# A two-layer diffusion backbone on one core: who forms h in the opening phase, and on which queue the later modulation weights are loaded

## The chip, the cores and the metric

The kernel runs on one core of one Trainium2 chip. The metric is the device time of one execution in microseconds (us): the median of several executions of the whole program. "About what can be told from no change" in the prediction means 1% of that time, some 15 us.

The core has five sequencers that run their own instruction lists in order and wait for each other through semaphores: TensorE (PE; its weight loads have a row of their own, PEld), VectorE (DVE), ScalarE (ACT), GpSimd (POOL) and SyncE (SP). DMAs are issued by SP, ACT or POOL, each on its own queue (SPq, ACTq, POOLq); a DMA that has to wait holds back everything behind it on the list of the engine that issues it.

## The reference, cut to what matters

Two layers work on 512 latent tokens (x) and 256 context tokens (ctx) of width 1024. The first thing that is computed is the adaptive norm of layer 0, then the first projections and the low-rank inputs of the RWKV branch:

```python
shift, scale, gate = jnp.split(s_lat @ mod_w[i] + mod_b[i], 3, axis=-1)
h = rms_norm(x, g_pre[i]) * (1.0 + scale[:, None]) + shift[:, None]
shift_c, scale_c, gate_c = jnp.split(s_ctx @ mod_w[i] + mod_b[i], 3, axis=-1)
hc = rms_norm(ctx, g_pre[i]) * (1.0 + scale_c) + shift_c
...
rc, kc, vc, zac, bc, cc, xc, zbc = jnp.split(hc @ w_in, EVEN_SPLITS, axis=-1)
r, k, v, za, bg, cg, xb, zb = jnp.split(h @ w_in, EVEN_SPLITS, axis=-1)
...
dh = centred_shift(h) - h            # 0.5 * (left + right) - h
xw = h + dh * mu_wa[0]
xa = h + dh * mu_wa[1]
lw = einsum(tanh(einsum(xw, w1)), w2)
la = einsum(einsum(xa, a1), a2)
```

After that come the bidirectional scan, a gated short convolution, the output projection, and layer 1 (a Conformer convolution module); neither is touched by the change.

## The kernel before, in words

**Precision.** Large products are made from split operands: `x = xh + xl`, where `xh` is `x` rounded to the matmul format fp32r and `xl` the rest. `mm3` (L59) runs three matmuls for one product: high by high (L60), high by low (L61), low by high (L62). So for each operand ScalarE casts the high part and another engine subtracts to get the low part; for weights that is `hilo` (L120: DMA, cast at L125, subtraction at L126 on the engine that `env["lo"]` names).

**The opening, `start()` (L208).** The columns of parameters are loaded on ACT's queue and transposed on PE. Six token tiles (two of ctx, four of x) are loaded on SP's queue (L226, L228). Then 16 loads of 512 KB bring the shift and scale parts of `mod_w` of layer 0 (L235, SP's queue) through six buffers (`mws`: four slices of the tile ectx, and mw4, mw5), each consumed by matmuls into the PSUM bank `mp` (L237). Meanwhile the tokens are normed (L242 to L245) and transposed into eight channel tiles `hp[kt]` (L253, L254), 770 columns each with zero columns for the shift at both ends of each stream. When `mp` is complete it is copied to SBUF (L256 on VectorE, L257 on ScalarE), transposed (L260, into `mt`), and gives the columns `modc0` (L261) and `gsc0` (L265). With them h is formed, first for ctx (8 tiles of 256 columns), then for the latents (8 of 512): the scaling of `hp[kt]` in place (L272 on ScalarE for odd latent tiles, L274 on VectorE for all others), the cast to the high part (L277, ScalarE; tile hctx or hlh), and the subtraction for the low part (L278, VectorE; tile hctx or hll).

**What follows.** `load_w(8, "k0")` (L839) loads the first projection weight (tile wrk, two halves of 256 KB) and splits it; for this one weight GpSimd does the subtraction (`lo_for`, L332). `start_w1` (L290) loads the low-rank weights (eight DMAs of 128 KB, L296) and four constants (L298 to L301). `prep_ctx(0, rest)` (L380) runs four projections (k0, k1, v0, v1): each a ctx product (`pck`, `pcv`: 24 matmuls of 256 columns) and a latent product (`plk`, `plv`: 24 of 512 columns), with the neighbour mix `shifted` behind each (L353 to L356). Between them `rest` (L847) works through the remaining 16 groups of modulation weights, which h does not need: four DMAs of 256 KB on POOL's queue (L856; tiles mwo, in the buffer that mw5 used, and mwr) and eight small matmuls into `uh` or `mpb` (L858). Then `lora` (L304): for each of eight channel tiles GpSimd adds the left and right neighbours (L310), VectorE forms `dh` (L311) and twice `xw = dh * mu + h` into one of four slots of the tile E1 (its name in the profile is ectx, L314), and PE multiplies each `xw` with its low-rank weight (`pwl`/`pal` and `pwc`, L317 and L318).

**What sets the order.** The code is traced in program order, and a scheduler of the framework then orders each engine's list by priority (program order) and by when it believes operands and buffers to be there. So a later piece can stand ahead of an earlier one on an engine's list: the matmuls of `rest` stand among those of `mp`, for example. `tc.issue_after(ins)` adds an edge, so that whatever the block traces on the engine of `ins` stands behind `ins` on that engine's list. `env["last"]` is, in the changed kernel, the last of the 16 `mod_w` DMAs of L235.

Of the kernel before, what the change touches and what calls it, by code (L numbers as in the profile page):

```python
# [10 lines left out]
AF = mybir.ActivationFunctionType  # L11
ALU = mybir.AluOpType
# [3 lines left out]
P = 128  # L16
D = 1024
# [34 lines left out]
def kernel(ctx: ExitStack, tc: tile.TileContext, I: dict, out: bass.AP):  # L52
# [129 lines left out]
    def small(name, shape):  # L182
        return cvp.tile(shape, F32, tag=name, name=name)

    ones = small("ones", [P, 1])
    G.memset(ones, 1.0)
    omu, hmu, hka, oka = (small(n, [P, k]) for n, k in (("omu", 24), ("hmu", 24), ("hka", 8), ("oka", 8)))
    blk = small("blk", [P, P])
    ctr = small("ctr", [P, P])
    maskE = small("maskE", [P, 3, P])  # L190
# [17 lines left out]
    def start():  # L208
        for gi, (grp, tag) in enumerate(zip(COLS, ("P", "kk", "kd", "a"))):
            rw = w(tag, f"rows{gi}")  # L210
            n_all = 0
            for nm, n in grp:
                src = colsrc[nm]
                while len(src.shape) > 1:
                    src = src.rearrange("a b -> (a b)" if len(src.shape) == 2 else "a b c -> (a b c)")
                nc.scalar.dma_start(rw[n_all : n_all + n, 0:P], src.rearrange("(a b) -> a b", b=P))
                n_all += n
            pt = ps_at(f"rowsT{gi}")
            T.transpose(pt[:, :n_all], rw[:n_all, 0:P], ident[:n_all, :n_all])
            V.tensor_copy(colt[gi], pt[:, :n_all])  # L220
            if gi == 0:
                S.activation(s2[:, :, 0], col("c", 0, 8), AF.Silu)
                S.activation(s2[:, :, 1], col("c_ctx", 0, 8), AF.Silu)
        tokt = [w("AR", f"tok{j}") for j in range(6)]
        for j in range(2):
            nc.sync.dma_start(tokt[j], I["ctx"][0, j * P : (j + 1) * P, :])  # L226
        for j in range(4):
            nc.sync.dma_start(tokt[2 + j], I["x"][0, j * P : (j + 1) * P, :])  # L228
        mws = [E1[:, D * q : D * q + D] for q in range(4)] + [w("X", "mw4"), w("O", "mw5")]
        mp = ps.tile([P, 512], F32, tag="zo", name="mp", bufs=2)  # L230
        V.memset(mp, 0.0)
        for kt in range(KT):
            for b in range(2):
                mw = mws[(2 * kt + b) % 6]
                nc.sync.dma_start(mw, I["mod_w"][0, kt * P : (kt + 1) * P, b * D : b * D + D])  # L235
                for q in (2 * b, 2 * b + 1):
                    mm(mp[32 * q : 32 * q + 2, :], s2[:, kt, :], mw[:, q % 2 * 512 : q % 2 * 512 + 512],  # L237
                       kt == 0, kt == KT - 1)
        hp = [w(t, f"hp{k}")[:, 0:D] for k, t in enumerate(("UV", "UV", "BKt", "BKt", "BKt", "BKt", "BK", "BK"))]
        for j in range(6):  # L240
            rs = ss6[:, 8 + j : 9 + j]
            S.activation(hp[7], tokt[j], AF.Square, accum_out=ss6[:, j : j + 1])  # L242
            S.activation(rs, ss6[:, j : j + 1], AF.Sqrt, bias=epsr[:, 0:1], scale=1.0 / D)
            V.reciprocal(rs, rs)
            V.tensor_scalar(out=tokt[j], in0=tokt[j], scalar1=rs, scalar2=None, op0=ALU.mult)  # L245
        for kt in range(KT):
            for c0, cn in ((0, 1), (257, 2), (771, 1)):
                G.memset(hp[kt][:, c0 : c0 + cn], 0.0)
        for kt in range(KT):
            for (j0, nj, o0) in ((0, 2, 1), (2, 4, 259)):  # L250
                pt = ps_mm(f"xt{kt}_{j0}")
                for j in range(nj):
                    T.transpose(pt[:, j * P : (j + 1) * P], tokt[j0 + j][:, kt * P : (kt + 1) * P], ident)  # L253
                S.copy(hp[kt][:, o0 : o0 + nj * P], pt[:, : nj * P])  # L254
        mrow = E1[:, 0:512]
        V.tensor_copy(mrow[:, 0:256], mp[:, 0:256])  # L256
        S.copy(mrow[:, 256:512], mp[:, 256:512])  # L257
        mt = ps_at("mt")
        for j in range(4):
            T.transpose(mt[:, j * P : (j + 1) * P], mrow[:, j * P : (j + 1) * P], ident)  # L260
        V.tensor_tensor(out=modc0.rearrange("p (q j) b -> p q j b", q=4),  # L261
                        in0=mt.rearrange("p (j q x) -> p q j x", j=4, q=4)[:, :, :, 0:2],
                        in1=col("mod_b0", 0, 16).rearrange("p (q j) -> p q j", q=4).unsqueeze(3).to_broadcast([P, 4, 4, 2]),
                        op=ALU.add)
        V.scalar_tensor_tensor(out=gsc0, in0=modc0[:, 8:16, :], scalar=1.0,  # L265
                               in1=col("g_pre0", 0, 8).unsqueeze(2).to_broadcast([P, 8, 2]),
                               op0=ALU.add, op1=ALU.mult)
        for (z, n, d0) in ((1, CTX, 1), (0, SEQ, 259)):
            for kt in range(KT):
                hv = hp[kt][:, d0 : d0 + n]  # L270
                if z == 0 and kt % 2:
                    S.activation(hv, hv, AF.Identity, scale=gsc0[:, kt, z : z + 1], bias=modc0[:, kt, z : z + 1])  # L272
                else:
                    V.tensor_scalar(out=hv, in0=hv, scalar1=gsc0[:, kt, z : z + 1],  # L274
                                    scalar2=modc0[:, kt, z : z + 1], op0=ALU.mult, op1=ALU.add)
                dh_, dl_ = (hch, hcl) if z else hlat
                S.copy(dh_[:, kt, :], hv)  # L277
                V.tensor_tensor(out=dl_[:, kt, :], in0=hv, in1=dh_[:, kt, :], op=ALU.subtract)  # L278
        V.tensor_scalar(out=omu, in0=col("mu_rkv", 0, 24), scalar1=-1.0, scalar2=1.0, op0=ALU.mult, op1=ALU.add)
        V.tensor_scalar(out=hmu, in0=col("mu_rkv", 0, 24), scalar1=0.5, scalar2=None, op0=ALU.mult)  # L280
        V.tensor_scalar(out=hka, in0=col("k_a", 0, 8), scalar1=0.5, scalar2=None, op0=ALU.mult)
        V.tensor_scalar(out=oka, in0=hka, scalar1=-1.0, scalar2=1.0, op0=ALU.mult, op1=ALU.add)
        ho = 0
        for nmh, nh in (("w0", 16), ("a0", 16), ("lnx_w", 8), ("lnx_b", 8), ("sc_w", 24)):
            V.tensor_scalar(out=hcol[:, ho : ho + nh], in0=col(nmh, 0, nh), scalar1=0.5, scalar2=None, op0=ALU.mult)
            half[nmh] = ho
            ho += nh
        return hp
# [15 lines left out]
    def lora(hp, w1, between):  # L304
        pwl, pal = (ps.tile([P, 512], F32, tag="zo", name=n, bufs=2) for n in ("pwl", "pal"))
        pwc = ps_at("pwc")
        for kt in range(KT):
            h1 = hp[kt][:, 1:771]
            dh = w("AR", f"dh{kt}")[:, 0:770]
            G.tensor_tensor(out=dh, in0=hp[kt][:, 0:770], in1=hp[kt][:, 2:772], op=ALU.add)  # L310
            V.scalar_tensor_tensor(out=dh, in0=dh, scalar=0.5, in1=h1, op0=ALU.mult, op1=ALU.subtract)  # L311
            for (zi, pl) in ((0, pwl), (1, pal)):
                xw = E1[:, (2 * kt + zi) % 4 * D : (2 * kt + zi) % 4 * D + 770]
                V.scalar_tensor_tensor(out=xw, in0=dh, scalar=col("mu_wa", zi * 8 + kt), in1=h1,  # L314
                                       op0=ALU.mult, op1=ALU.add)
                lhs = w1[zi][kt // 4][:, kt % 4].rearrange("p a b -> p (a b)")
                mm(pl, lhs, xw[:, 258:770], kt == 0, kt == KT - 1)  # L317
                mm(pwc[:, zi * CTX : (zi + 1) * CTX], lhs, xw[:, 0:CTX], kt == 0 and zi == 0, kt == KT - 1 and zi == 1)  # L318
            if kt % 2:
                between()  # L320
# [9 lines left out]
                V.tensor_tensor(out=lorl[i][z][lr], in0=t[rows], in1=th[rows], op=ALU.subtract)  # L330

    def lo_for(nm):  # L332
        env["lo"] = G if nm == "k0" else V

    def w_half(src, name):
        raw = wp.tile([P, 512], F32, tag="wr", name="wr" + name, bufs=2)
# [499 lines left out]
        nc.gpsimd.dma_start(ysp[8 + p], yb)  # L836

    hp = start()
    first_w = [load_w(8, "k0")]  # L839
    first = hp, start_w1()  # L840
    lorc_ = w("bon", "lorc")
    lorc = [lorc_[:, 0:CTX], lorc_[:, CTX : 2 * CTX]]
    mwo = w("O", "mwo")
# [3 lines left out]
    def rest(n=1):  # L847
        for g in range(mv["n"], min(mv["n"] + n, 16)):
            half_, kt = g // 8, g % 8
            if kt == 0:  # L850
                mv["acc"] = uhs[0] if half_ == 0 else ps.tile([P, 512], F32, tag="zo", name="mpb", bufs=2)
                V.memset(mv["acc"], 0.0)
            for q in range(4):
                u = 4 * half_ + q
                layer, c0 = (0, 2 * D + 512 * u) if u < 2 else (1, 512 * (u - 2))
                nc.gpsimd.dma_start(mws[q], I["mod_w"][layer, kt * P : (kt + 1) * P, c0 : c0 + 512])  # L856
            for q in range(4):
                mm(mv["acc"][32 * q : 32 * q + 2, :], s2[:, kt, :], mws[q], kt == 0, kt == KT - 1)  # L858
            if kt == KT - 1:
                rested(half_, mv["acc"])  # L860
        mv["n"] += n
# [410 lines left out]
```

## Time and profile before

| | us |
|---|---|
| median of 3 runs | 1514.84 |
| lowest, highest | 1505.89, 1517.57 |
| the profiled execution's own time | 1506.4 |
| its span (first to last instruction) | 1504.6 |
| mean granted TensorE clock in it | 0.978 of full |

The profile is of one execution. A row of the timeline reads: start (us from the span's start), duration, engine, source line, operation, out<-in by tile names, shapes, count; in square brackets, the idle time of the engine before it and what ended that. Neighbouring equal instructions are merged into one row with their count, and the duration then is from the first start to the last end. A row with a q behind the engine's name is the sequencer's, for instance a DMA being issued. A row of the table by stretches gives for each engine the busy time and in brackets the number of instructions, then the granted TensorE clock, the mean busy share of the 16 DMA engines, and GB/s. Durations of matmuls are modelled at their ends: pitches between starts are safer.

### The profile page before, as it was taken

Reading aid. Unit: us, or ns where it says so; the run is one execution under the profiler, and the core shown is the slowest. Engines: PE = TensorE matmul, PEld = TensorE weight load, DVE = VectorE, ACT = ScalarE, POOL = GpSimd, SP = SyncE. Lnnn points to the kernel's source line nnn. Section 1 sums busy time; section 2 is a strip of 40 time slices with the busy share of each in tenths; the row PEclk is TensorE's granted clock in tenths of the full one; section 3 lists DMA queues with packets and bytes.
Section 4 is the critical chain, followed back from the end, with each engine's and each line's share of the span. In section 5 each row is a group of like instructions: output and inputs, shape, how many; then the busy total and the mean of one; then the engine's idle time right before and its main releaser. Section 6 shows DMA issues by size and latency. Waiting matters only on the chain.

```text
span 1504.6 us, 29614 instructions
## 1 busy us (share of the span) xinstructions
PE 1429.3 (95%) x11857; PEld 1014.2 (67%) x11857; DVE 964.3 (64%) x2242; ACT 766.4 (51%) x1552; POOL 152.3 (10%) x263
## 2 busy tenths in 40 slices
PE   5699999999998999999999999999999999999998
PEld 1374577878776766666666666677757666688876
DVE  2575587558696978888788887658544525434333
ACT  4323465364755575755757657546553414363322
POOL 0533210000110101011011000001100000000000
PEclk9899999979997999999999999999999999999999
DMA  8644533212232312231222212468403303033222
GB/s 316 174 130 164 162 113 99 89 57 67 80 89 77 89 60 74 67 91 51 80 72 68 79 46 82 152 221 293 159 20 112 103 10 113 28 112 99 94 88 84
DMA packets 136650, 156.59 MB, mean 104 GB/s; under 512 B 15266, under 2 KB 104034, under 8 KB 136512
## 3 DMA queue, kind: packets, MB, share of 16 engines
q1 hardware_dynamic: 119952, 104.37, 22.4%
q0 software_dynamic: 15488, 49.14, 10.1%
q8 instruction: 93, 1.52, 0.4%
q10 hardware_dynamic: 1072, 1.19, 0.2%
q14 instruction: 45, 0.37, 0.1%
HBM read 137.36 MB, written 17.31 MB: 103 GB/s over the span
## 4 chain that ended last, share of the span: by engine, by line
PE 46%; ACT 6%; DVE 5%; DMA 2%; issue 2%; DVEq 0%; SPq 0%; ACTq 0%
PE pu L61 4%; PE pu L62 4%; PE pu L60 4%; PE zol L57 3%; PE uh L57 2%; PE f L61 2%; PE f L60 2%; PE f L62 2%; PE pz L61 2%; PE pz L62 2%; PE pz L60 2%; PE px L57 2%; PE pc L57 1%; PE pal L57 1%; PE o L62 1%
## 5 line engine op out<-in xcount | busy, mean ns | idle before, releaser
L57 PE MATMUL pal<-ARl,BKl 64*128 64x128 f32 x512 | 59.1, 311 | 6.3 <-DVE xtmpc L643 4.3
L645 DVE TENSOR_TENSOR Yl<-Yl,xtmpl 128x126 f32<-128x126 f32 (+22 forms) x248 | 62.5, 252 | 2.2
L643 DVE TENSOR_TENSOR xtmpl<-Xl,Yl 128x126 f32<-128x126 f32 (+22 forms) x248 | 62.4, 252 | 2.0
L57 PEld LDWEIGHTS pal<-ARl,BKl 64*128 64x128 f32 x512 | 44.2, 199 | 25.8 <-DVE E L588 6.2
L57 PE MATMUL zol<-UV,E 64*64 64x64 f32 (+1 forms) x1024 | 54.2, 221 | 0.0
L61 PE MATMUL o<-wl,y 128*128 128x512 f32 x124 | 50.0, 403 | 4.3 <-DVE wl L126 4.3
L57 PE MATMUL zol<-Hl,ARl 64*64 64x64 f32 x896 | 50.2, 230 | 2.3 <-DVE Hl L756 2.3
L1091 DVE TENSOR_TENSOR a<-pu,a 128x512 f32<-128x512 f32 x16 | 11.1, 692 | 62.0 <-PE pu L62 59.7
L749 ACT COPY UV<-uh 64x128 f32<-64x128 f32 x128 | 33.4, 261 | 33.2 <-PE uh L57 30.9
L126 DVE TENSOR_TENSOR wl<-wr,wh 128x1024 fp32r<-128x1024 f32 x28 | 37.1, 1323 | 20.7 <-ACT wh L125 20.5
L588 DVE TENSOR_TENSOR E<-pal,maskE 128x512 f32<-128x512 f32 x64 | 43.5, 685 | 10.4 <-PE pal L57 10.2
L60 PE MATMUL o<-wh,y 128*128 128x512 f32 x124 | 49.6, 401 | 0.5 <-ACT wh L125 0.5
L62 PE MATMUL o<-wh,y 128*128 128x512 f32 x124 | 49.9, 403 | 0.0
L57 PEld LDWEIGHTS zol<-Hl,ARl 64*64 64x64 f32 x896 | 35.0, 133 | 21.2 <-issue 16.9
L1096 ACT CAST ah<-a 64x512 fp32r<-64x512 f32 x32 | 19.8, 620 | 56.3 <-DVE a L1091 55.9
L756 DVE SCALAR_TENSOR_TENSOR Hl<-uh,PCl,HPl 128x64 f32<-128x64 f32 x112 | 26.8, 282 | 30.4 <-PE uh L57 21.4
L57 PEld LDWEIGHTS uh<-UV,BKt 128*64 128x64 f32 x704 | 26.8, 138 | 27.5 <-ACT UV L749 21.5
L57 PEld LDWEIGHTS zol<-UV,E 64*64 64x64 f32 (+1 forms) x1024 | 42.5, 136 | 2.8 <-ACT UV L749 2.1
L125 ACT CAST whcg<-wrcg 128x512 fp32r<-128x512 f32 x16 | 9.9, 621 | 63.5 <-DMA wrcg<-in_ev_w_in_dram 51.2
L57 PE MATMUL uh<-UV,BKt 128*64 128x64 f32 x704 | 36.9, 234 | 3.6 <-ACT UV L749 2.8
L125 ACT CAST wh<-wr 128x1024 fp32r<-128x1024 f32 x28 | 29.4, 1051 | 21.4 <-PE o L61 11.9
L57 PEld LDWEIGHTS uh<-Ol,E 64*64 64x64 f32 x512 | 19.9, 133 | 25.8 <-ACT Ol L743 17.4
(972 smaller groups left out, 4434.6 us busy)
## 6 DMA issues: line engine op xcount, KB each, us to landing
wr<-in_ev_w_out_dram SPq DMA_DIRECT2D x28, 512.0 KB, 5.0
mwr<-in_mod_w_dram POOLq DMA_DIRECT2D x32, 256.0 KB, 4.2
mwo<-in_mod_w_dram POOLq DMA_DIRECT2D x32, 256.0 KB, 3.2
ectx<-in_mod_w_dram SPq DMA_DIRECT2D x12, 512.0 KB, 5.1
wrk<-in_ev_w_in_dram SPq DMA_DIRECT2D x16, 256.0 KB, 2.9
wrv<-in_ev_w_in_dram SPq DMA_DIRECT2D x16, 256.0 KB, 2.9
wrr<-in_ev_w_in_dram SPq DMA_DIRECT2D x16, 256.0 KB, 2.9
wrza<-in_ev_w_in_dram SPq DMA_DIRECT2D x16, 256.0 KB, 2.8
```

The costliest lines, as they stand in the source:

```text
L57: return T.matmul(o, lhsT, rhs, start=start, stop=stop)
L60: T.matmul(o, ah, bh, start=start, stop=False)
L61: T.matmul(o, ah, bl, start=False, stop=False)
L62: T.matmul(o, al, bh, start=False, stop=stop)
L125: S.copy(hi, raw)
L126: env["lo"].tensor_tensor(out=lo, in0=raw, in1=hi, op=ALU.subtract)
L588: V.tensor_tensor(out=E[:, h, z * NLAT + c0 : z * NLAT + c0 + m, :], in0=pas[h], in1=maskE[:, z * (1 + h) : z * (1 + h) + 1, 0:x].to_broad ...
L643: V.tensor_tensor(out=tv, in0=X[:, :i, i : i + 1].to_broadcast([P, i, m]), in1=Y[:, i : i + 1, c0:].to_broadcast([P, i, m]), op=ALU.mult)
L645: V.tensor_tensor(out=Y[:, :i, c0:], in0=Y[:, :i, c0:], in1=tv, op=ALU.add)
L749: u_ = S.copy(UV[ZR[1 - h], i : 2 * nch - i : 2 * nch - 1 - 2 * i, ZR[h]], uh[ZR[1 - h], 0:2, :])
L756: h_ = V.scalar_tensor_tensor(out=Hn[:, z, :], in0=uh[:, 2 + z, :], scalar=PC[z][:, i : i + 1], in1=HP[:, z, :], op0=ALU.mult, op1=ALU.add)
L1096: S.copy(ahl[s][hr], a[hr])
```

## The change

Three things, all before the first stage of the scan. (1) In `start`, ScalarE writes the high part of h directly from `hp` (scale, bias and rounding in one ACTIVATE, 16 in all); VectorE then scales `hp` in place (all 16) and subtracts. The separate casts and the four ScalarE scalings in place are gone. (2) GpSimd's 8 additions (`dh`) go to VectorE, as does the subtraction for k0's weight; `dh` is now the sum of the two neighbours, `xw` is first `(1 - mu) * h` by ScalarE (16 new ACTIVATEs with the columns `owa`) and then `+ 0.5 * mu * dh` by VectorE. The 8 VectorE operations of L311 are gone, so that the number of VectorE operations in `lora` stays at 24. (3) The loads of k0's weight and of `start_w1` are tied behind the last `mod_w` DMA on SP's list, and the first two groups of `rest` (eight DMAs of 256 KB) are issued by SP, also behind it, instead of by POOL.

```diff
@@ start
+    owa, hwa = (small(n, [P, 16]) for n in ("owa", "hwa"))
...
-                nc.sync.dma_start(mw, I["mod_w"][0, kt * P : (kt + 1) * P, b * D : b * D + D])
+                env["last"] = nc.sync.dma_start(mw, I["mod_w"][0, kt * P : (kt + 1) * P, b * D : b * D + D])
...
                 hv = hp[kt][:, d0 : d0 + n]
-                if z == 0 and kt % 2:
-                    S.activation(hv, hv, AF.Identity, scale=gsc0[:, kt, z : z + 1], bias=modc0[:, kt, z : z + 1])
-                else:
-                    V.tensor_scalar(out=hv, in0=hv, scalar1=gsc0[:, kt, z : z + 1],
-                                    scalar2=modc0[:, kt, z : z + 1], op0=ALU.mult, op1=ALU.add)
                 dh_, dl_ = (hch, hcl) if z else hlat
-                S.copy(dh_[:, kt, :], hv)
+                S.activation(dh_[:, kt, :], hv, AF.Identity, scale=gsc0[:, kt, z : z + 1], bias=modc0[:, kt, z : z + 1])
+                V.tensor_scalar(out=hv, in0=hv, scalar1=gsc0[:, kt, z : z + 1],
+                                scalar2=modc0[:, kt, z : z + 1], op0=ALU.mult, op1=ALU.add)
                 V.tensor_tensor(out=dl_[:, kt, :], in0=hv, in1=dh_[:, kt, :], op=ALU.subtract)
...
+        V.tensor_scalar(out=owa, in0=col("mu_wa", 0, 16), scalar1=-1.0, scalar2=1.0, op0=ALU.mult, op1=ALU.add)
+        V.tensor_scalar(out=hwa, in0=col("mu_wa", 0, 16), scalar1=0.5, scalar2=None, op0=ALU.mult)
@@ lora
-            G.tensor_tensor(out=dh, in0=hp[kt][:, 0:770], in1=hp[kt][:, 2:772], op=ALU.add)
-            V.scalar_tensor_tensor(out=dh, in0=dh, scalar=0.5, in1=h1, op0=ALU.mult, op1=ALU.subtract)
+            V.tensor_tensor(out=dh, in0=hp[kt][:, 0:770], in1=hp[kt][:, 2:772], op=ALU.add)
             for (zi, pl) in ((0, pwl), (1, pal)):
                 xw = E1[:, (2 * kt + zi) % 4 * D : (2 * kt + zi) % 4 * D + 770]
-                V.scalar_tensor_tensor(out=xw, in0=dh, scalar=col("mu_wa", zi * 8 + kt), in1=h1,
+                S.activation(xw, h1, AF.Copy, scale=owa[:, zi * 8 + kt : zi * 8 + kt + 1])
+                V.scalar_tensor_tensor(out=xw, in0=dh, scalar=hwa[:, zi * 8 + kt : zi * 8 + kt + 1], in1=xw,
                                        op0=ALU.mult, op1=ALU.add)
@@ lo_for
-        env["lo"] = G if nm == "k0" else V
+        env["lo"] = V
@@ after start
-    first_w = [load_w(8, "k0")]
-    first = hp, start_w1()
+    with tc.issue_after(env["last"].ins):
+        first_w = [load_w(8, "k0")]
+        first = hp, start_w1()
@@ rest
+                if g < 2:
+                    with tc.issue_after(env["last"].ins):
+                        nc.sync.dma_start(mws[q], I["mod_w"][layer, kt * P : (kt + 1) * P, c0 : c0 + 512])
+                    continue
                 nc.gpsimd.dma_start(mws[q], I["mod_w"][layer, kt * P : (kt + 1) * P, c0 : c0 + 512])
```

## The prediction

> **What bounds the kernel now.** I read the page first, then the table by stretches of the opening, and then the timeline by engine around the places where PE idles.
>
> ```profile
> span 1504.6 us, 29614 instructions
> PE 1429.3 (95%) x11857; PEld 1014.2 (67%) x11857; DVE 964.3 (64%) x2242; ACT 766.4 (51%) x1552; POOL 152.3 (10%) x263
> PE   5699999999998999999999999999999999999998
> ```
>
> PE is busy nearly everywhere except in the first two of the 40 slices, that is in the first 75 us. The stretches say what kind of time that is (us; busy us of PE, PEld, DVE, ACT, POOL, each with a count; clock; DMA share; GB/s):
>
> ```profile
> 20.00:40.00 20.00, 19.59 (x92) 5.92 (x88) 4.34 (x9) 9.38 (x24) 0.79 (x5) 1.00 0.91 328
> 55.90:63.00 7.10, 1.92 (x5) 0.46 (x4) 7.06 (x20) 6.95 (x15) 3.02 (x6) 0.94 0.84 249
> 63.00:69.00 6.00, 5.94 (x25) 5.74 (x26) 6.00 (x4) 1.67 (x4) 6.00 (x4) 0.50 0.01 1
> 69.00:76.00 7.00, 4.18 (x17) 2.83 (x16) 7.00 (x8) 2.65 (x5) 3.65 (x3) 0.99 0.00 0
> 84.70:135.00 50.30, 50.30 (x223) 31.86 (x224) 30.04 (x40) 9.75 (x17) 18.08 (x24) 1.00 0.47 151
> ```
>
> From 84.7 to 135 PE has no idle time and its clock is full: it works off the projections and lora, and what comes earlier into that stretch comes out of it earlier. Before it PE waits for h, and h waits for the modulation columns. The chain, on PE and the issuing queues:
>
> ```profile
> 1.85 1.25 POOL L856 DMA_DIRECT2D mwr<-in_mod_w_dram  x2 [0.27 <-issue]
> 31.06 5.29 SPq L235 DMA_DIRECT2D ectx<-in_mod_w_dram  x4
> 36.40 0.98 SPq L122 DMA_DIRECT2D wrk<-in_ev_w_in_dram  x2
> 39.38 1.07 POOL L856 DMA_DIRECT2D mwo<-in_mod_w_dram  x2 [13.00 <-PE mp L57]
> 39.59 1.03 PE L57 MATMUL mp<-ectx,s 128*2 128x512 f32 x4
> 45.79 1.01 PE L57 MATMUL uh<-mwo,s 128*2 128x512 f32 x1 [4.60 <-DMA mwo<-in_mod_w_dram]
> 48.84 1.04 PE L57 MATMUL mp<-ectx,s 128*2 128x512 f32 x5
> 51.46 1.02 PE L57 MATMUL uh<-mwo,s 128*2 128x512 f32 x2 [1.57 <-DMA mwo<-in_mod_w_dram]
> 52.41 0.66 PE L260 MATMUL mt<-ident,ectx 128*128 128x128 f32 x4
> 63.06 0.80 PE L60 MATMUL plk<-hlh,whk 128*128 128x512 f32 x1 [3.86 <-ACT hlh L277]
> 77.65 0.63 PE L61 MATMUL plk<-hll,whk 128*128 128x512 f32 x1
> 78.08 0.63 PE L62 MATMUL plk<-hlh,wlk 128*128 128x512 f32 x1
> ```
>
> Twice a matmul of `rest` (uh), which nobody needs yet, stands on PE's list ahead of what h needs and waits for its own DMA: at 45.79 ahead of the last matmuls of `mp`, at 51.46 ahead of the transposes mt. The mod_w loads themselves were all issued by 36.4.
>
> VectorE carries h from there, up to the last subtraction at 75.47:
>
> ```profile
> 49.94 0.42 DVE L256 COPY ectx<-mp 128x256 f32<-128x256 f32 x1 [22.32 <-DMA maskE<-in_maskE_dram]
> 50.40 0.37 ACT L257 COPY ectx<-mp 128x256 f32<-128x256 f32 x1 [8.57 <-DVE ectx L256]
> 53.10 0.19 DVE L261 TENSOR_TENSOR modc<-mt,cols 128x32 f32<-128x32 f32 x1 [2.74 <-PE mt L260]
> 53.33 2.63 DVE L265 SCALAR_TENSOR_TENSOR gsc<-modc,cols 128x16 f32<-128x16 f32 x1
> 53.41 2.50 POOL L126 TENSOR_TENSOR wlk<-wrk,whk 128x512 fp32r<-128x512 f32 x2
> 55.99 1.49 DVE L274 TENSOR_SCALAR hp<-hp,gsc,modc 128x256 f32<-128x256 f32 x4
> 61.38 0.53 DVE L274 TENSOR_SCALAR hp<-hp,gsc,modc 128x512 f32<-128x512 f32 x1
> 61.84 0.68 DVE L278 TENSOR_TENSOR hll<-hp,hlh 128x512 fp32r<-128x512 f32 x1
> 62.44 1.72 DVE L274 TENSOR_SCALAR hp<-hp,gsc,modc 128x512 f32<-128x512 f32 x1
> 62.42 6.83 POOL L310 TENSOR_TENSOR dh<-hp 128x770 f32<-128x770 f32 x4 [2.18 <-DVE hp L274]
> 64.09 5.71 DVE L278 TENSOR_TENSOR hll<-hp,hlh 128x512 fp32r<-128x512 f32 x3
> 75.47 0.68 DVE L278 TENSOR_TENSOR hll<-hp,hlh 128x512 fp32r<-128x512 f32 x1
> ```
>
> The reader is to see that VectorE stretches whenever GpSimd computes: 16 columns of gsc take 2.63 us beside wlk on POOL, where modc with 32 columns took 0.19; a 512-wide scaling takes 1.72 beside dh against 0.53 alone; three subtractions take 5.71 against 0.68 each. This agrees with the Trainium skill, GPSIMD Engine Reference, Key points, which has the two share SBUF interfaces when VectorE reads two SBUF inputs or runs a 2-port mode.
>
> **The change part by part.** The sum is made against the profiled execution's own 1506.4 us (span 1504.6 and 1.8 around it).
>
> *Step A, the end of mp.* The last four mod_w issues begin at 31.06, the last at 36.0, and a mod_w load lands 5.1 us behind its issue:
>
> ```profile
> L235 SPq DMA_DIRECT2D ectx<-in_mod_w_dram x12: 327/328/432, 12.7 to 36.0; - x12
> DMA to landing us min/median/max: 5.1/5.1/5.1
> ```
>
> So the last is there at 41.1; I take 41.5, since wrk and the low-rank weights follow at once on the same queue and still do. A group of four mp matmuls takes 1.03, with 0.5 for hand-offs mp ends at 43.0 in place of 48.84 + 1.04 = 49.9: **6.9 us gained**, if PE's new order has uh behind mp. I take that, because uh's loads now stand behind wrk, the low-rank weights and the constants on SP, hence later than mp's in any order by readiness. Bounds: 0 (something else not ready stands there), and 8.5 (the 0.5 MB that POOL loads at 1.85 are out of the way: 1.6 us at 328 GB/s, left out since the early matmuls of mp wait for more than data).
>
> The part of the change that ties wrk and the low-rank weights behind mod_w does nothing by itself: on SPq they already are (36.40 behind 31.06 + 5.29). What moves is the eight loads of `rest`: they cost SP eight issues more, some 3.5 us by 1.07 for two on POOL, behind everything h needs. The second four wait on SP for PE to have read the first four (same buffers); behind them wait the issues of k1's and v0's weights. That costs nothing while PE runs uh in its gaps before k0's product ends (the stretch 55.9 to 63 has 5 us of idle PE), and some 6 us once (issue, landing, cast, subtraction) if PE puts uh behind k0.
>
> The Trainium skill, DMA: Bandwidth & Descriptors, Queues, rings and completion order, has each DMA engine alternate between the queues that have work; by it POOL's two early loads take their share from SP's, and step A would be larger; that is the rival "more than forecast".
>
> *Step B, from mp to gsc:* 49.88 to 55.96, 6.1 us. Left are the two copies (0.9 with hand-off, 49.94 to 50.77), 0.3 to PE, the transposes (52.41 to 53.10, 0.7), modc 0.2, gsc 0.2: 2.3. **Gained 3.8**: 1.57 from uh at 51.46, the rest from gsc without POOL beside it.
>
> *Step C, from gsc to the end of k0's products:* 55.96 to 78.71, 22.75 us. VectorE has the same 16 pairs of scaling and subtraction as ever and four more scalings. At paces without POOL: ctx 55.99 to 61.38, 5.4 for eight pairs; a latent pair 61.38 to 62.44, 1.06, eight make 8.5; k0's two weight subtractions, taken over from POOL, 0.6 each by their pitch, 1.2 (61.84 to 62.44). ScalarE's form with fp32r output does not occur in the trace; the rows nearest are the same ACTIVATE with float output and the cast:
>
> ```profile
> L272 ACT ACTIVATE hp<-hp,modc,gsc 128x512 f32<-128x512 f32 x4 | 3.1, 811 | 4.2 <-DVE gsc L265 4.2
> L277 ACT CAST hlh<-hp 128x512 fp32r<-128x512 f32 x8 | 4.7, 616 | 6.7 <-DVE hp L274 6.7
> ```
>
> It lies between 0.62 (a cast alone) and 1.43 (both in a row); I take 0.81, as the arithmetic is that of L272. Then ScalarE, at no more than 16 x 0.81 = 13.0, stays under VectorE's 5.4 + 8.5 = 13.9, and only its first, some 0.6 for half the columns, is on the path; at 1.43 for a latent tile and about 0.8 for a ctx tile it would need 18 and cost 4 us. In-place scaling now waits for ScalarE to have read, which runs ahead. PE's tail behind the last subtraction: 1.0. Sum 5.4 + 8.5 + 1.2 + 0.6 + 1.0 = 16.7: **gained 6.0**.
>
> PE's clock was 0.50 from 63 to 69, behind the 3.86 us wait, and full again from 69. In my sum PE's gaps until k0's end are shorter than that wait, so it is costed at full clock; at half clock it is a rival, below. The Trainium skill, TensorE: Matmul & The Clock Gate, Part 1, states the rule behind these rows, and it speaks against a PE that is fed in drops: half rate after an idle window of some 3.4 us, until a window of as long is busy.
>
> *Step D, lora and behind.* VectorE's 8 operations of L311 become 8 additions of the same width, cost as before; they no longer wait for POOL.
>
> ```profile
> L311 DVE SCALAR_TENSOR_TENSOR dh<-dh,hp x8: 944/948/961, 76.5 to 92.6; 128x770 f32<-128x770 f32 x8
> 115.13 1.02 PE L57 MATMUL pal<-ectx,a 128*128 128x512 f32 x2
> 116.42 1.02 PE L57 MATMUL pwl<-ectx,w 128*128 128x512 f32 x2
> 115.33 1.02 DVE L314 SCALAR_TENSOR_TENSOR ectx<-dh,cols,hp 128x770 f32<-128x770 f32 x1 [0.24 <-PE pwc L57]
> ```
>
> ScalarE gets 16 ACTIVATEs of 770 columns, 0.9 to 1.1 each by the 0.81 for 512; it is busy 9.75 of 50.3 there, so they fit (about 16). Each xw slot goes round in ScalarE 1.0, VectorE 1.0, PE 1.29 and three hand-offs of 0.25, about 4.0 us; with four slots that is 1.0 per unit against PE's 1.29 (115.13 to 116.42), so PE still sets the pace: nothing. One uh group (0.97) that ran in an idle PE now runs in a busy one, and a stall of about that size at 84 goes. Net 0, bounds -2 and +2.
>
> Sum: 6.9 + 3.8 + 6.0 = 16.7, rounded down to 16.5 for the new ops in between: 1506.4 - 16.5 = 1489.9 for an execution like the profiled one. The median shown is 1514.84, 8.4 above it; the median forecast is 1514.8 - 16.5 = **1498.3 us**.
>
> **The rivals.**
>
> *The wait moves on PE's list.* The order is made by estimates of readiness. Evidence for: at 63.06 k0's first latent matmul stood ahead of its ctx ones and held PE 3.86 us, besides the two waits for uh. If one such wait stays, 3.9 to 8 us are kept: gain 8.5 to 12.6, about 1504.
>
> *VectorE becomes the bound.* It takes all of POOL's arithmetic. If the scheduler pulls the eight additions ahead of the latent subtractions, h is later by 8 x 0.95 = 7.6: gain 9, 1506. Against: h is earlier in program order.
>
> *PE stays at half clock.* Fed tile by tile, PE may not count as busy. At half clock a 512-column matmul starts every 0.43 (77.65 to 78.08), so a latent tile's three take 1.29 against VectorE's 1.06: 8 x 0.23 = 1.8 us more and a longer tail, 0.6. Gain 14.1, 1500.7. Against: in the stretch 55.90:63.00 PE was busy 1.92 of 7.10 us at clock 0.94.
>
> *Mod_w does not land earlier, so step A is not there.* If the descriptors behind the last load, not PE's order, hold it until about 45.5, A shrinks to 2 to 3: gain 12, 1503.
>
> *More than forecast.* The 0.5 MB that POOL loads at 1.85 no longer stand ahead of mod_w; at the 328 GB/s of the stretch from 20 that is 1.6 us, and 2 us in D come on top: gain 20, 1495.
>
> *Slower: the slots of lora.* ScalarE writes a slot first and VectorE then completes it; if fewer than the four slots are in flight, because an xw on ScalarE's in-order list is held behind a cast that waits for a weight, the round of 4.0 us shows. With two in flight it is 2.0 per unit, 16 x 0.7 = 11 us, which still leaves a gain; with one, 16 x 2.7 = 43 us and a net loss of 27, 1541. It decides below about 1.8 slots. Against: in the trace four are in flight (the xw at 115.33 follows the pwc four units earlier), and ScalarE is idle four fifths of the time.
>
> **How the numbers follow.** The forecast 0.36; PE at half clock 0.08; PE's order 0.22; VectorE 0.11; mod_w's landing 0.06; more than forecast 0.11; lora slower 0.06. A measurement of this kernel can tell about 1%, 15 us, from no change, and the forecast lies just across that line: of its 0.36 some 0.30 are over 1%, with all of "more", 0.03 of half clock and 0.04 of the others; slower by over 1% is lora's 0.06. So faster 0.48, same 0.46, slower 0.06. The likeliest case alone spans 1493 to 1504. The range takes in the other gains (1509) and the single execution's level at the low end (1490 and a little less): 1487 to 1510.
>
> **What would show it.** The last mp matmul at 43 in place of 49.9, with no DMA wait of uh ahead of it; gsc at 0.2 us, at about 45.5; latent pairs on VectorE at 1.06 throughout; no POOL arithmetic before 100 us; the last k0 matmul near 62; PE without a gap from there to the end of lora, near 118. I would be wrong if PE shows a new wait of over 3 us before k0's end, if VectorE does additions of 770 columns between the latent subtractions, or if PE waits for ScalarE's xw in lora.

## The result and the profile after

The changed kernel takes 1492.43 us (median of 4 runs, 1483.60 to 1499.09) against 1510.37 for the kernel before (4 runs, 1504.58 to 1517.57): a ratio of 0.9887, with a 95% interval of 0.984 to 0.9934. The interval leaves out 1 but holds 0.99, so there is a gain, and whether it is over 1% stays open. The forecast was 1498.3 us with 16.5 gained; 17.9 separate the medians. The profiled execution of the changed kernel is its slowest run, 1499.09 us, so the two traces lie only 7 us apart; a section below says where the other 9 went.

The page of the changed kernel:

```profile
span 1497.3 us, 29614 instructions
PE 1433.0 (96%) x11857; PEld 1014.5 (68%) x11857; DVE 957.5 (64%) x2250; ACT 779.7 (52%) x1564; POOL 125.9 (8%) x245
PE   5999999999989999999999999999999999999998
```

The second slice of PE, which was 6, is 9. The table by stretches of the changed kernel (columns as before: us; busy us of PE, PEld, DVE, ACT, POOL with counts; clock; DMA share; GB/s):

```profile
41.90:44.20 2.30, 0.84 (x4) 0.40 (x4) 1.35 (x5) 1.42 (x4) 0.00 (x0) 1.00 0.87 197
44.20:52.00 7.80, 6.83 (x27) 6.13 (x28) 7.70 (x21) 7.80 (x14) 0.00 (x0) 0.56 0.94 279
52.00:61.30 9.30, 8.88 (x35) 4.13 (x33) 8.76 (x17) 6.60 (x10) 0.35 (x1) 1.00 0.41 130
61.30:76.00 14.70, 14.70 (x89) 10.52 (x88) 12.25 (x17) 4.05 (x7) 2.87 (x6) 1.00 0.77 224
76.00:120.00 44.00, 44.00 (x192) 26.14 (x189) 25.47 (x32) 19.82 (x28) 13.61 (x26) 1.00 0.48 159
```

From the end of mp to that of k0's products POOL does next to nothing, VectorE is busy 17.8 of 19.4 us, ScalarE 15.8 and PE 16.6. Behind it PE has no gap up to 120, past the end of lora. In the timeline of the changed kernel the chain of the prediction reads:

```profile
29.14 5.29 SPq L236 DMA_DIRECT2D ectx<-in_mod_w_dram  x4
34.48 0.99 SPq L122 DMA_DIRECT2D wrk<-in_ev_w_in_dram  x2
40.84 1.03 PE L57 MATMUL mp<-ectx,s 128*2 128x512 f32 x4 [0.60 <-DMA ectx<-in_mod_w_dram]
42.40 0.84 PE L261 MATMUL mt<-ident,ectx 128*128 128x128 f32 x4 [0.53 <-DVE ectx L257]
43.98 0.17 DVE L266 SCALAR_TENSOR_TENSOR gsc<-modc,cols 128x16 f32<-128x16 f32 x1
48.14 5.74 ACT L273 ACTIVATE hlh<-hp,modc,gsc 128x512 fp32r<-128x512 f32 x8
51.28 0.99 DVE L274 TENSOR_SCALAR hp<-hp,gsc,modc 128x512 f32<-128x512 f32 x2
52.20 1.28 DVE L276 TENSOR_TENSOR hll<-hp,hlh 128x512 fp32r<-128x512 f32 x2
58.48 0.68 DVE L276 TENSOR_TENSOR hll<-hp,hlh 128x512 fp32r<-128x512 f32 x1
60.90 0.40 PE L62 MATMUL plk<-hlh,wlk 128*128 128x512 f32 x1
```

No `uh` matmul is left ahead of mp or mt; the last four matmuls of mp wait 0.60 us for their own data. gsc takes 0.17 in place of 2.63, and two latent pairs take 2.12 from 51.28 to 53.40, where the next scaling starts, 1.06 each, as forecast. k0's products end at 61.3 in place of 78.7.

### The profile page after: what moved, and what is told of

It reads as the page before. It is cut to its first block, busy times and chain, and to the rows that moved or that the text cites. A ratio compares the mean times of both kernels' runs of the same rounds, so it can differ in the third digit from the quotient of the medians.

```text
span 1497.3 us, 29614 instructions
## 1 busy us (share of the span) xinstructions
PE 1433.0 (96%) x11857; PEld 1014.5 (68%) x11857; DVE 957.5 (64%) x2250; ACT 779.7 (52%) x1564; POOL 125.9 (8%) x245
## 4 chain that ended last, share of the span: by engine, by line
PE 44%; ACT 7%; DVE 5%; DMA 4%; issue 2%; SPq 0%; DVEq 0%; ACTq 0%
PE pu L61 4%; PE pu L62 4%; PE pu L60 4%; PE zol L57 3%; PE uh L57 2%; PE f L61 2%; PE f L62 2%; PE f L60 2%; PE pz L62 2%; PE pz L61 2%; PE pz L60 2%; PE px L57 2%; PE pal L57 1%; PE pc L57 1%; DMA wrcg<-in_ev_w_in_dram 1%
## 5 line engine op out<-in xcount | busy, mean ns | idle before, releaser
L57 PEld LDWEIGHTS pal<-ARl,BKl 64*128 64x128 f32 x512 | 44.2, 199 | 25.9 <-DVE E L588 6.1
L1096 DVE TENSOR_TENSOR a<-pu,a 128x512 f32<-128x512 f32 x16 | 11.1, 691 | 61.6 <-PE pu L62 59.3
L62 PE MATMUL o<-wh,y 128*128 128x512 f32 x124 | 49.9, 403 | 0.0
L57 PEld LDWEIGHTS zol<-Hl,ARl 64*64 64x64 f32 x896 | 35.1, 133 | 21.3 <-issue 17.1
L756 DVE SCALAR_TENSOR_TENSOR Hl<-uh,PCl,HPl 128x64 f32<-128x64 f32 x112 | 26.6, 280 | 30.7 <-PE uh L57 21.6
```

The source lines that it names most:

```text
L57: return T.matmul(o, lhsT, rhs, start=start, stop=stop)
L62: T.matmul(o, al, bh, start=False, stop=stop)
L756: h_ = V.scalar_tensor_tensor(out=Hn[:, z, :], in0=uh[:, 2 + z, :], scalar=PC[z][:, i : i + 1], in1=HP[:, z, :], op0=ALU.mult, op1=ALU.add)
```

## Experiments

Ten kernels were run. Six of them take the three parts of the change singly and in pairs. Times of one kernel spread by 10 to 20 us, so a ratio (the time against that of the kernel before, with its 95% interval) is good to about 0.004 (6 us) here; the landmarks of the trace separate what the medians can't. Each landmark comes from one execution; the last two rows, which are the same work in the same order, differ by 0.3 us at most. "lora's end" is the end of the last matmul of lora, the gain is against 132.7 in the profile of before, and "PE idle" is PE's idle time in the gaps that begin between 18 us and lora's end.

| kernel | parts | mp ends | gsc ends | k0's products end | lora's end (gain) | PE idle | ratio, interval |
|---|---|---|---|---|---|---|---|
| before | none | 49.9 | 56.0 | 78.7 | 132.7 | 15.9 | |
| e2_act_only | 1 | 49.9 | 55.3 | 80.4 | 135.1 (-2.4) | 17.0 | 1.0035, 0.999 to 1.008 |
| e3_nopool_only | 2 | 49.4 | 52.5 | 73.7 | 122.9 (9.8) | 7.9 | 0.9905, 0.9876 to 0.9934 |
| e1_queue_only | 3 | 42.1 | 44.9 | 68.1 | 127.7 (5.0) | 11.2 | 0.9985, 0.9945 to 1.0024 |
| e4_no_queue | 1, 2 | 49.3 | 52.8 | 79.5 | 129.2 (3.5) | 9.5 | 0.9983, 0.9955 to 1.001 |
| e5_no_poolpart | 1, 3 | 41.2 | 43.9 | 67.4 | 123.5 (9.2) | 8.2 | 0.9941, 0.991 to 0.9972 |
| e6_no_act | 2, 3 | 40.9 | 43.2 | 58.6 | 118.4 (14.3) | 5.1 | 0.991, 0.9877 to 0.9944 |
| after | 1, 2, 3 | 41.9 | 44.2 | 61.3 | 116.9 (15.8) | 3.9 | 0.9887, 0.984 to 0.9934 |
| e8_no_tie | 1, 2, 3 | 42.2 | 44.5 | 61.6 | 117.1 (15.6) | 4.4 | 0.9914, 0.988 to 0.9948 |

**Part 3 alone (e1_queue_only).** From the changed kernel, parts 1 and 2 are undone:

```diff
-                S.activation(dh_[:, kt, :], hv, AF.Identity, scale=gsc0[:, kt, z : z + 1], bias=modc0[:, kt, z : z + 1])
+                S.copy(dh_[:, kt, :], hv)
...
+                if z == 0 and kt % 2:
+                    S.activation(hv, hv, AF.Identity, scale=gsc0[:, kt, z : z + 1], bias=modc0[:, kt, z : z + 1])
+                else:
                     V.tensor_scalar(out=hv, in0=hv, scalar1=gsc0[:, kt, z : z + 1],
                                     scalar2=modc0[:, kt, z : z + 1], op0=ALU.mult, op1=ALU.add)
...
-            V.tensor_tensor(out=dh, in0=hp[kt][:, 0:770], in1=hp[kt][:, 2:772], op=ALU.add)
+            G.tensor_tensor(out=dh, in0=hp[kt][:, 0:770], in1=hp[kt][:, 2:772], op=ALU.add)
+            V.scalar_tensor_tensor(out=dh, in0=dh, scalar=0.5, in1=h1, op0=ALU.mult, op1=ALU.subtract)
-                S.activation(xw, h1, AF.Copy, scale=owa[:, zi * 8 + kt : zi * 8 + kt + 1])
-                V.scalar_tensor_tensor(out=xw, in0=dh, scalar=hwa[:, zi * 8 + kt : zi * 8 + kt + 1], in1=xw,
+                V.scalar_tensor_tensor(out=xw, in0=dh, scalar=col("mu_wa", zi * 8 + kt), in1=h1,
-        env["lo"] = V
+        env["lo"] = G if nm == "k0" else V
```

> The kernel before with part 3 alone: the first two groups of rest on SP, tied behind the last mod_w load; h and lora as before, GpSimd computing. Marks: mp's last matmul ended at 49.9 before and 41.9 after, lora's last matmul at 132.2 before and 116.3 after. Theory (the uh matmuls on PE's list held mp back; worth 8 us, and 1.6 ahead of mt): mp ends at 42, lora near 122, gain 9 to 12. Rival one (h is bound by VectorE beside GpSimd, whenever the columns come): mp ends at 42 but lora near 130, gain under 4. Rival two (mod_w lands late because of its own queue): mp still ends at 46 or later.

Lora's end gains 5.0 us, between the theory's 9 to 12 and the under 4 of rival one. The columns come nearly as early as in the full change (gsc 11.1 us earlier than before), but h then takes 20.7 us (44.9 to the last subtraction at 65.6) in place of 15.0. On VectorE of e1_queue_only, and on POOL beside it:

```profile
52.77 1.70 DVE L275 TENSOR_SCALAR hp<-hp,gsc,modc 128x512 f32<-128x512 f32 x1
54.39 1.95 DVE L279 TENSOR_TENSOR hll<-hp,hlh 128x512 fp32r<-128x512 f32 x1
57.87 5.71 DVE L279 TENSOR_TENSOR hll<-hp,hlh 128x512 fp32r<-128x512 f32 x3
63.50 0.54 DVE L275 TENSOR_SCALAR hp<-hp,gsc,modc 128x512 f32<-128x512 f32 x1
63.96 0.68 DVE L279 TENSOR_TENSOR hll<-hp,hlh 128x512 fp32r<-128x512 f32 x1
```

```profile
50.82 12.21 POOL L313 TENSOR_TENSOR dh<-hp 128x770 f32<-128x770 f32 x6 [4.72 <-DVE hp L275]
```

While POOL's additions run, from 50.8 to 63.0, a scaling takes 1.70 and a subtraction 1.9; from 63.50, with POOL idle, they are back at 0.54 and 0.68. PE stands behind them, in the table of waits of this kernel from 44 to 80:

```profile
PE plk L61 <- DVE hll L279: 5.1, 1, 5.1
PE pck L60 <- ACT hctx L278: 3.2, 1, 3.2
```

**Parts 1 and 2 alone (e2_act_only, e3_nopool_only)**, made from the edits above and by taking part 3 out:

```diff
-    with tc.issue_after(env["last"].ins):
-        first_w = [load_w(8, "k0")]
-        first = hp, start_w1()
+    first_w = [load_w(8, "k0")]
+    first = hp, start_w1()
...
-                if g < 2:
-                    with tc.issue_after(env["last"].ins):
-                        nc.sync.dma_start(mws[q], I["mod_w"][layer, kt * P : (kt + 1) * P, c0 : c0 + 512])
-                    continue
```

> The kernel before with part 1 alone: ScalarE forms the high parts of h directly, VectorE does all 16 scalings; GpSimd's additions and POOL's loads as before. Theory (VectorE beside GpSimd bounds h, and it gets four scalings more): nothing gained, lora ends between 131 and 134. Rival (the two steps in place, scaling then cast, were the delay): 5 us gained, lora ends near 127.

> The kernel before with part 2 alone: dh and k0's weight subtraction on VectorE, the first step of xw on ScalarE; h and the queues as before. Theory (GpSimd's work stretches VectorE's): gsc takes 0.2 in place of 2.6, the latent pairs run at 1.06, lora ends near 124, gain 7 to 9. Rival (work moved to VectorE costs what the stretching cost): gain under 3, lora at 130 or later.

Both went the way of the theory and somewhat past its ranges. ScalarE's form alone gains nothing: lora ends 2.4 us later (at 135.1, where 131 to 134 was expected), the ratio holds 1. POOL's work moved to VectorE gains 9.8 us at lora's end (7 to 9 was expected) and is the largest single part; how much of it the additions, k0's subtraction and the new form of `xw` bring each was not separated. It gains this though mp still ends at 49.4: PE goes on waiting for `uh`'s weights (table of waits of e3_nopool_only, 20 to 123 us):

```profile
PE uh L57 <- DMA mwo<-in_mod_w_dram: 6.2, 4, 4.1
```

**Pairs (e4_no_queue, e5_no_poolpart, e6_no_act)**: the changed kernel with one part undone by the same edits: e4_no_queue by the diff just above, e5_no_poolpart by the lines of the diff of e1_queue_only from `dh` on, e6_no_act by those ahead of it.

> The changed kernel without part 3: parts 1 and 2 alone, the loads of rest all on POOL. Theory (parts are additive: 8 to 10 us belong to the queue part): mp ends at 49 to 50, lora ends near 124 to 126, gain 6 to 8. Rival (with GpSimd free of arithmetic, POOL issues early enough that uh no longer holds mp): mp ends at 44 or before, lora within 2 us of 116.3.

> The changed kernel without part 2: parts 1 and 3, GpSimd doing the eight additions and k0's weight subtraction as before. Lora's last matmul ended at 132.7 before, at 116.9 after, at 127.7 with part 3 alone, at 122.9 with part 2 alone. Theory (GpSimd beside VectorE stretches h, whatever the columns' time): h takes over 20 us from gsc to its last subtraction against 15 after, lora ends at 126 to 130. Rival (part 1 takes the pressure off VectorE, so that GpSimd no longer matters): lora ends at 120 or before.

> The changed kernel without part 1: parts 2 and 3, h formed as before (ScalarE scaling four latent tiles in place, separate casts). Theory (part 1 adds four scalings to VectorE, which bounds h, and takes a cast off the way of each tile: about even): lora ends at 115.5 to 119, the total within 0.3% of the changed kernel's 0.9887. Rival (part 1 carries a share of the gain on top of the others): lora ends at 121 or later.

e6_no_act shows that part 1 is worth at most 1.5 us at lora's end beside the other two; the ratios (0.991 and 0.9887) don't tell them apart. h itself is even formed sooner without it, 12.5 us from gsc to the last subtraction (43.2 to 55.7) against 15.0, and k0's products end at 58.6 against 61.3; this is lost again behind them, with 59.8 us to lora's end against 55.6. e5_no_poolpart ended between the two expectations, with the mechanism of the theory: h takes 22.7 us (43.9 to 66.6). e4_no_queue went against the theory that the parts add up: parts 1 and 2 together gain 3.5 at lora's end, less than part 2 alone. Its table of waits, 20 to 130 us, and its PE:

```profile
PE uh L57 <- DMA mwo<-in_mod_w_dram: 8.4, 4, 4.9
```

```profile
72.42 0.59 PE L57 MATMUL uh<-mwo,s 128*2 128x512 f32 x1
72.43 0.59 PE L57 MATMUL uh<-mwr,s 128*2 128x512 f32 x1
72.85 0.59 PE L57 MATMUL uh<-mwo,s 128*2 128x512 f32 x1
72.86 0.59 PE L57 MATMUL uh<-mwr,s 128*2 128x512 f32 x1
73.38 0.50 PE L61 MATMUL plk<-hll,whk 128*128 128x512 f32 x1
```

POOL waits with the loads of `rest`, PE waits 8.4 us for them, and up to lora's end the `uh` products stand on PE's list in 21 pieces, against 15 in e3_nopool_only and 11 in the full change. Here a piece of two products (each product is two records) holds PE from 72.42 to 73.38, 0.96 us; adding the pitches up, `uh` costs PE 20.4 us to lora's end, against 15.8 and 11.7.

**The edge itself (e8_no_tie)**: the changed kernel without the edge around k0's weight and the low-rank weights. The order on each engine's list stays the same.

```diff
-    with tc.issue_after(env["last"].ins):
-        first_w = [load_w(8, "k0")]
-        first = hp, start_w1()
+    first_w = [load_w(8, "k0")]
+    first = hp, start_w1()
```

> The change without its edge that puts k0's weight and the low-rank weights behind the last mod_w DMA (the first eight loads of rest keep theirs). Theory: the lists of the five engines are the same with and without the edge, so this is the change once more: mp ends between 41 and 43, gsc at 44, k0's products at 61, lora at 117, ratio 0.985 to 0.992. What differs from the profile of the change is then what one kernel's executions differ by: the number and the places of the stretches at half clock behind 200 us. Rival: the edge does something that the lists do not show (a semaphore on SP's list that delays or keeps apart the loads); then mp ends outside 41 to 43 or the first matmuls of k0 or lora wait for a weight, by 1 us or more.

It is the change once more: 1492.40 us (11 runs, 1485.09 to 1497.39), all landmarks within 0.3 us. So that part of the change does nothing that these runs can tell, as forecast; its use here is that it shows the same lists in another execution.

**The 0.5 MB at the front (e7_early_mwr)**, one execution: the first two loads of `mwr` go back to POOL's queue, at the start of the kernel.

```diff
-                if g < 2:
+                if g == 1 or g == 0 and q < 2:
```

> The changed kernel with only the first two mwr loads (0.5 MB) back on POOL, where they are issued at 2 us; the lists of PE and VectorE are the same. Theory (DMA bandwidth sets the pace of the first 42 us, so 0.5 MB ahead of mod_w cost 1.6 us): mp ends at 43.5 in place of 41.9 and every later mark moves by as much. Rival (PE's order and the buffers set the pace): mp ends within 0.3 us of 41.9.

```profile
32.44 5.29 SPq L236 DMA_DIRECT2D ectx<-in_mod_w_dram  x4
43.84 1.03 PE L57 MATMUL mp<-ectx,s 128*2 128x512 f32 x4 [0.30 <-DMA ectx<-in_mod_w_dram]
```

mp ends at 44.9, 3.0 us later than in the change, and lora 2.6 later; its one time was 1484.21. That is more than 0.5 MB at 328 GB/s, but it isn't conclusive: the start of the last four mod_w issues lies between 28.95 and 30.34 in the seven kernels that load these tiles on SP, at 29.63, 29.89, 30.17 and 31.06 in the four that load them early on POOL, and at 32.44 here. The two groups overlap; their means differ by 0.6 us without e7_early_mwr.

**Whole groups (e10_whole)**: after e4_no_queue the four products of a group of `rest` were tied together on PE's list.

```diff
-            for q in range(4):
-                mm(mv["acc"][32 * q : 32 * q + 2, :], s2[:, kt, :], mws[q], kt == 0, kt == KT - 1)
+            go = pinned()
+            for q in (3, 2, 1, 0):
+                go(mv["acc"][32 * q : 32 * q + 2, :], s2[:, kt, :], mws[q], kt == 0, kt == KT - 1)
```

> The changed kernel with the four products of each group of rest in a fixed order, last loaded first, so that they stand together on PE's list. In the traces four products that stand together take 0.97 us and a single one 0.95, as they use different columns of PE; the changed kernel has them in 10 runs until lora's end, at a cost of 11.7 us, the one without part 3 in 17 to 21 runs, at 20.4 us. Theory (pieces of groups cost PE time that lora's end sees): the cost falls to 7.5, lora ends at 112.5 to 114, ratio near 0.986. Rival (the pieces lie in time in which PE would wait anyway): lora within 1 us of 116.9.

```profile
93.26 0.60 PE L57 MATMUL uh<-mwr,s 128*2 128x512 f32 x2
93.28 0.60 PE L57 MATMUL uh<-mwo,s 128*2 128x512 f32 x2
93.69 0.60 PE L57 MATMUL uh<-mwr,s 128*2 128x512 f32 x2
93.70 0.60 PE L57 MATMUL uh<-mwo,s 128*2 128x512 f32 x2
94.23 1.13 PE L57 MATMUL pwl<-ectx,w 128*128 128x512 f32 x2
```

Four products together hold PE 0.97 us (93.26 to 94.23), as long as two did in e4_no_queue, and `uh` falls from 11.7 to 9.5 us. k0's products end at 60.4, where the change has 61.3. Nothing of it reached lora's end, which comes at 120.7, later than either expectation: the new order of the list has a wait of its own (table of waits, 42 to 121 us), so that the theory stays untested. The ratio is 0.9913, interval 0.9879 to 0.9946.

```profile
PE plv L60 <- DVE lk L356: 3.0, 1, 3.0
```

**Scaling shared (e9_share)**: ScalarE scales the odd latent tiles in place again, beside writing all high parts.

```diff
+                if z == 0 and kt % 2:
+                    S.activation(hv, hv, AF.Identity, scale=gsc0[:, kt, z : z + 1], bias=modc0[:, kt, z : z + 1])
+                else:
                     V.tensor_scalar(out=hv, in0=hv, scalar1=gsc0[:, kt, z : z + 1],
                                     scalar2=modc0[:, kt, z : z + 1], op0=ALU.mult, op1=ALU.add)
```

> The change, with one thing moved back to ScalarE: of the latent tiles the four odd ones are scaled in place by ScalarE (as before the change), so VectorE has 12 scalings and 16 subtractions. Theory: with gsc at 44 VectorE sets the pace of h in the latent tiles (1.06 a pair), so four scalings of 0.5 less bring the last subtraction about 1.5 to 2 us forward, from 59.2 to 57.5; the end of k0's products comes from 61.1 to about 59.5 and the end of lora from 116.9 to 115.5; the time is then 1.5 us under that of the change, which five rounds can hardly tell from nothing (ratio 0.986 to 0.991 against the kernel before). Rival: ScalarE, with 0.72 for a high part and 0.8 for a scaling, has 1.5 us for an odd tile and becomes what PE waits for, so that the end of k0's products stays at 61 or comes later, and the end of lora is 117 or later.

k0's products end at 61.2, lora at 117.1: the rival's numbers, but not its mechanism. VectorE's four scalings are gone, and in the middle of the latent tiles stands an addition of lora instead (timeline of VectorE of e9_share):

```profile
53.78 0.95 DVE L313 TENSOR_TENSOR dh<-hp 128x770 f32<-128x770 f32 x1
54.65 1.28 DVE L279 TENSOR_TENSOR hll<-hp,hlh 128x512 fp32r<-128x512 f32 x2
57.91 0.68 DVE L279 TENSOR_TENSOR hll<-hp,hlh 128x512 fp32r<-128x512 f32 x1
```

The last subtraction ends 0.6 us earlier than in the change, but PE has no time to win: it idles 3.7 us to lora's end, where the change has 3.9. The median was 1486.93 (6 runs), the ratio 0.9887, interval 0.9843 to 0.9931, which overlaps that of the change's lists on the same chip (e8_no_tie, 0.9914, interval 0.988 to 0.9948); whether it is faster stays open.

## Why the prediction was right

The theory of the prediction (two `uh` waits on PE's list and POOL beside VectorE make h late) stands, against the rivals that one of these waits stays or that VectorE becomes the bound: with part 3 alone the two waits are gone and mp ends at 42.1, and without part 2 h takes over 20 us, whatever else is changed. By its own steps:

*Step A, 6.9 forecast, 8.0 measured* (49.9 to 41.9). From the first of the last four mod_w issues to the end of mp the prediction had 11.9 us (31.06 to 43.0); the changed kernel took 12.7 (29.14 to 41.87), and e8_no_tie 12.0 (30.24 to 42.19). What was mis-sized is the start of these issues, which the prediction left at 31.06: it came 1.9 us earlier. That belongs to its rival "more than forecast", but e8_no_tie has the same lists and began them at 30.24, 1.1 us later than the changed kernel, and the two groups of kernels overlap. How much of the 1.9 is the 0.5 MB and how much is the execution stays open. The rule of the Trainium skill named there (DMA: Bandwidth & Descriptors, Queues, rings and completion order) is thus neither borne out nor contradicted.

*Step B, 3.8 forecast, 3.8 measured*: 2.3 us from mp's end to gsc's (41.87 to 44.15).

*Step C, 6.0 forecast, 5.6 measured*: 17.15 us from 44.15 to 61.30, with 16.7 forecast. h itself took 15.0 of them, where the terms add up to 15.7, but the tail of PE behind the last subtraction took 2.1 us (59.16 to 61.30), and 1.0 was taken for it. The prediction let `uh` run in PE's gaps here at no cost, but a piece of it stands on PE's list ahead of that subtraction's product:

```profile
59.62 1.02 PE L57 MATMUL uh<-mwo,s 128*2 128x512 f32 x2
60.57 0.50 PE L61 MATMUL plk<-hll,whk 128*128 128x512 f32 x1
```

In e10_whole, where no such piece stands there, the tail is 0.8 us (59.59 to 60.37). ScalarE's high parts cost 0.72 each (5.74 for eight) where 0.81 was taken, so ScalarE is not the bound. The rival "PE at half clock" was right that the clock falls, and wrong about the place: it was 0.50 for 6.8 us from 44.8, in the ctx products (the stretch 44.20:52.00 has 0.56), where VectorE's pair takes 0.66 and PE's three half-clock matmuls 0.64; nearly all latent products ran at full clock. It cost nothing that shows: e8_no_tie had only 3.4 us at half clock there and took the same 17.15.

*Step D, 0 with bounds of 2 either way; -1.6 measured*: 55.6 us from k0's end to lora's against 54.0. PE is busy throughout and waits for no slot of lora, so the slower rival did not come about. Only 10 records of `uh` lie ahead of k0's end where 18 did; what had run in PE's gaps now runs in a full PE, and `uh` costs 8.8 us of pitches behind k0's end where it cost 6.1. That this makes the 1.6 us is argued from these figures.

The sum, 8.0 + 3.8 + 5.6 - 1.6 = 15.8 at lora's end, stands against 16.5. That it comes so close is in part luck, as the steps miss by +1.1, -0.4 and -1.6. So is the nearness of the medians: the interval allows a gain of 10 to 24 us, and the same lists in e8_no_tie gave 0.9914, some 13 us. The 1498.3 itself stood on a level of 1514.84 for the kernel before, which came out at 1510.37.

Singly the three parts gave -2.4, 9.8 and 5.0, together 15.8. Part 3 removes the wait for the columns, part 2 the stretched VectorE, and these two are nearly the whole: 14.3 together, where their single gains add up to 14.8. What doesn't add up is part 1: it is worth -2.4 alone, 4.2 beside part 3, -6.3 beside part 2, and 1.5 beside both.

**Where the gain goes behind lora.** The first operation of the scan's solve on VectorE comes 15.3 us earlier; the kernel before, then the changed one:

```profile
182.09 0.22 DVE L643 TENSOR_TENSOR xtmpc<-Xc,Yc 128x31 f32<-128x31 f32 x1
```

```profile
166.75 0.19 DVE L643 TENSOR_TENSOR xtmpc<-Xc,Yc 128x31 f32<-128x31 f32 x1
```

The first matmuls of the latent scan (tile zol, 1024 of one kind; first and last start) come only 10.0 us earlier in the profile of the change, and 15.8 in that of e8_no_tie with the same lists; before, after and e8_no_tie:

```profile
L57 PE MATMUL zol<-UV,E x1024: 218/222/271, 537.8 to 989.0; 64*64 64x64 f32 x86, 128*64 128x64 f32 x85
```

```profile
L57 PE MATMUL zol<-UV,E x1024: 218/222/270, 527.8 to 979.6; 64*64 64x64 f32 x86, 128*64 128x64 f32 x85
```

```profile
L57 PE MATMUL zol<-UV,E x1024: 217/221/271, 522.0 to 973.6; 64*64 64x64 f32 x86, 128*64 128x64 f32 x85
```

The difference goes with the clock. Two stretches at half clock of 20 us and more fall into the scan of ctx in each of the three: at 322 and 455 in before (20.5 us each), at 306 and 439 in e8_no_tie (20.5 each), but at 212 (20.5) and 441 (30.7) in the changed kernel's profile; from before and after:

```profile
322.00:342.00 20.00, 20.00 (x150) 17.52 (x147) 6.25 (x11) 6.78 (x16) 0.00 (x0) 0.50 0.13 41
```

```profile
212.00:232.00 20.00, 20.00 (x102) 15.06 (x102) 4.93 (x9) 5.84 (x11) 1.07 (x2) 0.50 0.25 79
322.00:342.00 20.00, 19.56 (x248) 15.99 (x248) 14.28 (x43) 10.62 (x27) 0.54 (x1) 1.00 0.13 41
```

Paired by instruction, the changed kernel leads by 15.4 us up to 200, by 6.4 from 250 on (its stretch cost 9), by 14.5 from 350 (the one of before cost 8), and by 10 from 500 (10 us more at half clock cost 4.5); between 950 and 1050, where PE waits for weights, it falls to 7. e8_no_tie leads by about 15.8 throughout to 950 us and by 13.8 at the end. So the gain of the opening is carried through, and the 9 us that the profiled pair lacks lie in stretches that the change doesn't touch: some 5 in the places of the half clock, some 3 where PE waits for weights.

## What to carry to other kernels

Cost a change as a chain up to the point from which the bounding engine has no more gaps, and test its parts singly and in pairs: here gsc came 11.1 us earlier by part 3 alone and lora's end only 5.0, two of the parts added up, and the third ranged from -6.3 to 4.2 with what stood beside it. A product that nobody needs yet, loaded on another queue, can hold an in-order list twice; queue its load behind what is needed and its place on the list moves with it. And follow a gain landmark by landmark through the trace before believing a median, since here one stretch of half clock cost 9 us, more than half of what the change gains.

## What the runs showed of the hardware

- Stretches at half clock of 17.1 to 30.7 us occur in the scan in each of the twelve profiles. Those at 322 in the kernel before and at 212 in the changed one persist although PE is then busy 20.00 of 20.00 us. Just before the one at 212 PE had been busy 5.58 of 7.00 us, but that alone doesn't bring one on: e8_no_tie had 5.60 of 7.00 there and kept the full clock. The changed kernel, then e8_no_tie (two rows):

```profile
205.00:212.00 7.00, 5.58 (x47) 3.72 (x46) 6.00 (x10) 6.89 (x15) 0.55 (x1) 1.00 0.26 80
```

```profile
205.00:212.00 7.00, 5.60 (x47) 3.77 (x48) 5.60 (x9) 6.89 (x15) 1.61 (x3) 1.00 0.24 78
212.00:232.00 20.00, 20.00 (x203) 15.00 (x203) 12.12 (x26) 9.62 (x21) 0.55 (x1) 1.00 0.41 118
```

- What sets these stretches off stays open. All lengths seen (3.4, 6.8, 17.1, 20.5, 23.9, 30.7) are multiples of 3.4, but for the stretch in which each profile ends. The Trainium skill (TensorE: Matmul & The Clock Gate, Part 1) gives windows of about that length, which agrees, and full rate after one busy window, which these stretches do not show. Over the runs of the kernel before, 1500 us went with a mean clock of 0.982 and 1515 with 0.971.
- Products with two columns, put in four column groups, run side by side only when adjacent on PE's list: 0.95 us for one (54.52 to 55.47 in the changed kernel), 0.96 for two (72.42 to 73.38 in e4_no_queue), 0.97 for four (93.26 to 94.23 in e10_whole). The Trainium skill (TensorEngine Tiling (Array Packing), Key Properties) states that tiles operate independently, and the trace agrees; scattered pieces threw that away (20.4 us for `uh` in 21 pieces in e4_no_queue, 9.5 in 8 pieces in e10_whole).
